# A wider recurrence, a moved product and a later turning in the mixer of a decoder layer

## The chip, the cores and the metric

The kernel runs on one core of a Trainium2 chip. The metric is the device time of one launch in microseconds (us), the median of several runs. Profiles come from one profiled execution. TensorE does the matrix products (PE; its weight loads are shown as PEld), VectorE (DVE) and ScalarE (ACT) the elementwise work, GpSimd (POOL) a few clearings and sums, and SyncE (SP) issues nearly all transfers.

## The reference

One layer of a decoder over 512 tokens of width 2048, all float32. After an RMSNorm one projection feeds three mixers, whose outputs are joined, projected and added; then a SwiGLU block of hidden width 5632 and a last RMSNorm.

```
h = rms_norm(x, attn_norm_g);  proj = h @ w_in
ya = diff_attention(...)            # 4 heads, two softmaxes each, causal
yb = sliding_window_attention(...)  # 8 heads, window 128, sinks
feats = token_shift(rw, mu)         # 16 heads of 64
kk = kk / max(norm(kk), 1e-12);  k = k * (1 + (a - 1) * k_a)
step:  S = S * w_t + (S @ a_t) b_t' + v_t k_t';  y_t = S r_t     # a_t = -kk, b_t = kk * a
x = x + concat(ya, yb, yc) @ w_out
x = x + (silu(gate) * up) @ w_down
return rms_norm(x, final_norm_g)
```

## The kernel before

**Dense work.** Every projection works on tiles of 128 output features by 512 tokens. Its weights come in 512 KB pieces (`raw`), are rounded on ScalarE to a high part (`wh`, L207) and on VectorE to the rest (`wl`, L208), and three matmuls a step (L130) make the product. The weights of a projection are loaded while the one before it runs. Projections go in a fixed order: r, k, v for eight pairs of heads (k first), then q, k, v for four attention heads, with `kb` and `vb` of the window attention ahead of the third head, then `qb`, then the output projection `po` and the feed-forward block (`pg`, `pu`, `pd`).

**Lanes and the planner.** The mixers' own instructions are written as generators in lanes. After each dense matmul `pump` lets each lane whose due time has come go on by one piece. Due times are in the planner's own time `self.now`, which each matmul advances by an estimate; `charge` adds up estimated VectorE and ScalarE time in `self.free` and `self.last`. A bare `yield` means "when the last piece should be done, plus `slack`", `yield 2.5` means 2.5 us of planned time later. TensorE's order is exactly the order so written. VectorE's and ScalarE's order is set by a scheduler by priority, in which `high_priority` moves instructions ahead. Where the next dense projection needs a tile whose older content is still to be used, `need` lets only the lanes run until it is free.

**A pair's way.** For each pair of heads hp:

- `rates`: decay and rate tiles `W`, `V` (`IW`), `a`.
- `prep`: the norm of kk (`kn` matmul), kk (L512), `ar[:, :, 0]` (L518), kk*a (L521), two writes of `bk` (L526), a*k (L527), two more (L531). Then it waits until `loop{hp-2}` is done (the gate, L534), transposes `bk` on TensorE (`bt`, L134) into `bkn`, takes r, writes `ar[:, :, 1]` (L547), and forms the masked products `gr`, `zl` and `L` (`linv`, L574). `ar` has two buffers, so that of pair hp is the one of pair hp-2. The diagonal 32x32 blocks of `L` go to memory (`li`, L585).
- `inverse`: 32 blocks come back, one in each of 32 partitions as a 32x32 matrix `x` (L621). Thirty steps of two VectorE instructions (L629, L630) invert them all. ScalarE makes the transposed copy `xtt` (L633), and both go to memory (`xi`, `xj`).
- `join`: the inverses come back into `L` (L649), two transposed ones into `xn` (L651); two rounds of small matmuls (`pt`, `po`) and ScalarE copies fill the off-diagonal block.
- `chain` (named `loop{hp}`): eight chunks in sequence, each with z, u, S and y matmuls and copies between them. Then `post` (named `chain{hp}`).

The next pair's `prep` begins when the one before is done, and a loop begins when the y tile of the one before is free. Two tiles are released late: the dense v of pair hp may be stored only when v of pair hp-1 has been used up.

**Attention.** `diff_head` begins with `chain7` done. For each of four blocks `scores` makes two score matmuls (`sa`), softmax on VectorE and ScalarE into `pa`; `turned` transposes it on TensorE (`wt`); `values` multiplies (`oa`). Blocks are staggered: `scores(blk + 2)` is issued after `turned(blk)`. A tile of the third head's q may be stored only when head 0 is done.

Of the kernel before, what the change touches and what calls it, by code (L numbers as in the profile page):

```python
# [8 lines left out]
F32 = mybir.dt.float32  # L9
F32R = mybir.dt.float32r  # L10
AF = mybir.ActivationFunctionType
ALU = mybir.AluOpType
AX = mybir.AxisListType

P = 128
T = 512
# [3 lines left out]
C = 64  # L20
NCH = T // C
# [67 lines left out]
class Kernel:  # L89
    def __init__(self, tc, ins, out, dbg=None, stop=None):  # L90
        self.tc = tc
        self.nc = tc.nc
        self.i = ins
        self.out = out
        self.dbg = dbg or {}
        self.stop = stop
        self.lanes = [[], [], [], [], [], [], [], []]
        self.order = [self.lanes[j] for j in (2, 7, 6, 5, 0, 1, 3, 4)]
        self.done = set()
        self.flags = set()  # L100
        self.now = 0.0
        self.due = {}
        self.free = {"DVE": 0.0, "Activation": 0.0}
        self.last = 0.0
        self.slack = 0.3

    def col(self, name, j=0, n=P):
        c = COL[name] + j
# [384 lines left out]
    def prep(self, hp):  # L493
        nc, rp = self.nc, self.rp
# [5 lines left out]
        k = q["k"]  # L500
# [4 lines left out]
        ps = self.pm.tile([P, T], F32, tag="m", name=f"kn{hp}")  # L505
        self.mm(ps, self.cst("onesbd", P), rn, start=True, stop=True)
        kk = rp.tile([P, T], F32, tag="kk", name=f"kk{hp}")

        nc.scalar.activation(kk, ps, AF.Relu, bias=self.cst("knmin", 1))
        nc.scalar.activation(kk, kk, AF.Ln, bias=self.cst("kneps", 1))  # L510
        nc.scalar.activation(kk, kk, AF.Exp, scale=-0.5)
        nc.vector.scalar_tensor_tensor(out=kk, in0=k, scalar=kk_g, in1=kk, op0=ALU.mult, op1=ALU.mult)  # L512

        def c3(x):
            return x.rearrange("p (n c) -> p n c", c=C)

        ar = rp.tile([P, NCH, 2, C], F32, tag="ar", name=f"ar{hp}", bufs=2)
        nc.vector.scalar_tensor_tensor(out=ar[:, :, 0, :], in0=c3(kk), scalar=-1.0, in1=W[:, :, 0:64],  # L518
                                       op0=ALU.mult, op1=ALU.mult)
        bk = rp.tile([P, NCH, 2, C], F32, tag="bk", name=f"bk{hp}")  # L520
        nc.vector.tensor_tensor(out=kk, in0=kk, in1=a, op=ALU.mult)  # L521
        nc.scalar.activation(a, a, AF.Identity, bias=self.one_less("k_a", hp), scale=self.col("k_a", hp))

        for h in range(2):
            s = slice(h * 64, h * 64 + 64)
            nc.vector.tensor_tensor(out=bk[s, :, h, :], in0=c3(kk)[s], in1=V[s, :, 1:65], op=ALU.mult)  # L526
        nc.vector.tensor_tensor(out=a, in0=a, in1=k, op=ALU.mult)  # L527
        self.done.add(f"k{hp}")
        for h in range(2):
            s = slice(h * 64, h * 64 + 64)  # L530
            nc.vector.tensor_tensor(out=bk[s, :, 1 - h, :], in0=c3(a)[s], in1=V[s, :, 1:65], op=ALU.mult)  # L531
        yield

        while hp >= 2 and f"loop{hp - 2}" not in self.done:  # L534
# [9 lines left out]
        while "r" not in q:  # L544
            yield
        r = q["r"]
        nc.vector.tensor_tensor(out=ar[:, :, 1, :], in0=c3(r), in1=W[:, :, 1:65], op=ALU.mult)  # L547

        nc.vector.tensor_tensor(out=a, in0=a, in1=r, op=ALU.mult)
# [63 lines left out]
    def inverse(self, q):  # L613

        nc, rp = self.nc, self.rp
        hp = q["hp"]
        yield 2.5


        x = rp.tile([32, 32, 32], F32, tag="i2", name="x")  # L620
        nc.sync.dma_start(out=x, in_=q["li"].rearrange("h b n s t -> (h b n) s t"))  # L621
        yield 2.5
        nc.vector.memset(x.rearrange("p s t -> p (s t)")[:, 0:1024:33], 1.0)
        tmp = rp.tile([32, 32, 32], F32, tag="i3", name="xt")
        for j in range(1, 31):
            n = 31 - j
            cl = x[:, j:j + 1, j + 1:32].to_broadcast([32, j, n])
            rw = x[:, 0:j, j:j + 1].to_broadcast([32, j, n])
            nc.vector.tensor_tensor(out=tmp[:, :j, :n], in0=cl, in1=rw, op=ALU.mult)  # L629
            nc.vector.tensor_tensor(out=x[:, 0:j, j + 1:32], in0=x[:, 0:j, j + 1:32], in1=tmp[:, :j, :n], op=ALU.add)  # L630
            yield max(self.free["DVE"] - self.now - 1.0, 0.1)
        xt = rp.tile([32, 32, 32], F32, tag="i1", name="xtt")
        nc.scalar.copy(out=xt[0:32].rearrange("p t s -> p s t"), in_=x)  # L633
        d = self.dp.tile([2, 2, NCH, 32, 32], F32, name=f"xi{hp}")
        dt = self.dp.tile([2, 2, NCH, 32, 32], F32, name=f"xj{hp}")
        nc.sync.dma_start(out=d.rearrange("h b n s t -> (h b n) s t"), in_=x)
        nc.sync.dma_start(out=dt.rearrange("h b n t s -> (h b n) t s"), in_=xt)
        q.update(xi=d, xj=dt)
        self.lanes[7].append((f"inv{hp}", self.join(q)))
        yield  # L640

    def join(self, q):

        nc, rp = self.nc, self.rp
        hp, L, blocks, d, dt = (q[n] for n in ("hp", "L", "blocks", "xi", "xj"))
        yield 4.5
        xn = rp.tile([P, NCH, 32], F32, tag="xn", name="xnn")
        for h, b, bl in blocks:
            nc.sync.dma_start(out=L[bl, :, bl], in_=d[h, b].rearrange("n s t -> s n t"))  # L649
            if not b:  # L650
                nc.sync.dma_start(out=xn[bl], in_=dt[h, b].rearrange("n t s -> t n s"))  # L651
        yield 3

        ps = self.pc.tile([P, NCH, 32], F32, tag="c", name="pt")
        for n in range(NCH):
            for h in range(2):
                lo, hi = blocks[2 * h][2], blocks[2 * h + 1][2]
                self.mm(ps[hi, n, :], L[lo, n, hi], xn[lo, n, :], start=True, stop=True)
        pt = rp.tile([P, NCH, 32], F32, tag="pt", name="pts")
        for h in range(2):  # L660
            hi = blocks[2 * h + 1][2]
            nc.scalar.copy(out=pt[hi], in_=ps[hi])
        yield
        ps = self.pc.tile([P, NCH, 32], F32, tag="c", name="po")
        for n in range(NCH):
            for h in range(2):
                lo, hi = blocks[2 * h][2], blocks[2 * h + 1][2]
                self.mm(ps[lo, n, :], pt[hi, n, :], L[hi, n, hi], start=True, stop=True)
        for h in range(2):
            lo, hi = blocks[2 * h][2], blocks[2 * h + 1][2]  # L670
            nc.scalar.copy(out=L[lo, :, hi], in_=ps[lo])
        yield
        self.lanes[2].append((f"loop{hp}", self.chain(q)))
# [165 lines left out]
    def diff_head(self, h, q, vtag):  # L839
# [5 lines left out]
        while "k" not in q:  # L845
            yield
        qT, kT = q["q"], q["k"]
        ws = {}

        def scores(blk):  # L850
            nk = (blk + 1) * P
            ps = [self.pm.tile([P, T], F32, tag="m", name=f"sa{h}_{blk}_{c}") for c in range(2)]
            for c in range(2):
                s = slice(c * 64, c * 64 + 64)
                self.mm(ps[c][:, :nk], qT[s, blk * P:(blk + 1) * P], kT[s, :nk])
            p = rp.tile([P, 2, T], F32, tag=("bk", "i1")[blk % 2], name=f"pa{h}_{blk}")
            st = rp.tile([P, 8], F32, tag="st", name=f"st{h}_{blk}", bufs=3)
            for c in range(2):
                nc.vector.tensor_tensor_reduce(out=p[:, c, :nk], in0=ps[c][:, :nk], in1=bias[:, T - nk:], scale=1.0,
                                               scalar=-3e38, op0=ALU.add, op1=ALU.max, accum_out=st[:, c:c + 1])  # L860
            nc.vector.tensor_scalar(out=st[:, 2:4], in0=st[:, 0:2], scalar1=-1.0, scalar2=None, op0=ALU.mult)
            for c in range(2):
                nc.scalar.activation(p[:, c, :nk], p[:, c, :nk], AF.Exp, bias=st[:, 2 + c:3 + c],
                                     accum_out=st[:, 4 + c:5 + c])
            nc.vector.reciprocal(out=st[:, 6:8], in_=st[:, 4:6])
            nc.vector.tensor_tensor(out=st[:, 7:8], in0=st[:, 7:8], in1=self.nlam, op=ALU.mult)
            nc.vector.tensor_scalar(out=p[:, 1, :nk], in0=p[:, 1, :nk], scalar1=st[:, 7:8], scalar2=None, op0=ALU.mult)
            nc.vector.scalar_tensor_tensor(out=p[:, 0, :nk], in0=p[:, 0, :nk], scalar=st[:, 6:7], in1=p[:, 1, :nk],
                                           op0=ALU.mult, op1=ALU.add)
            ws[blk] = p  # L870

        def turned(blk):
            p = ws[blk]
# [21 lines left out]
        for blk in range(4):  # L895
            turned(blk)
            back = self.last + self.slack - self.now
            if blk:
                values(blk - 1)
            if blk < 2:  # L900
                scores(blk + 2)
            yield back
        values(3)
        o = rp.tile([P, T], F32, tag="sq2", name=f"osq{h}")
        nc.scalar.activation(o, po, AF.Square)
# [371 lines left out]
```

## Time and profile before

| | us |
|---|---|
| median of 3 runs | 2482.63 (2481.53 to 2483.27) |
| profiled execution, its own time | 2481.82 |
| its span | 2480.0 |
| PE busy in the span | 2419.3 |
| DVE busy | 1230.6 |
| ACT busy | 824.2 |

Rows of groups give: line, engine, operation, output <- input by the program's names, shape, count, then busy time, mean ns of one, and idle time before with what ended it. Rows of waits give who waited for whom, us in total, times, longest. Rows in order of time give start, duration, engine, operation, and in brackets the idle time just before with its releaser. A matmul in plain float32 leaves two records. The granted clock is that of TensorE, 1.00 being full speed.

### The profile page before, as it was taken

How to read it: one execution, taken by the hardware profiler on the slowest of the kernel's cores; microseconds unless marked ns; L12 is line 12 of the kernel's file. 1: busy time of each engine (PE TensorE's matmuls, PEld its weight loads, DVE VectorE, ACT ScalarE, POOL GpSimd, SP SyncE). 2: the span in 40 equal slices, each digit the busy share in tenths (PEclk: the TensorE clock that was granted, in tenths of full speed). 3: DMA queues.
4: the chain of work that ended last, by engine and by line, in shares of the span. 5: the costliest groups of instructions: out<-in, count | busy, mean ns of one | idle time of the engine just before them, and what ended most of it. 6: DMA issues, size and time to landing. Idle time of an engine off the chain costs nothing.

```text
span 2480.0 us, 30228 instructions
## 1 busy us (share of the span) xinstructions
PE 2419.3 (98%) x12072; PEld 1921.0 (77%) x12072; DVE 1230.6 (50%) x2113; ACT 824.2 (33%) x1383; POOL 93.0 (4%) x117
## 2 busy tenths in 40 slices
PE   8999999989999999999999999999999999999997
PEld 6776666667677778888888888888888888888887
DVE  7587777776454544434343434343434334343437
ACT  5454555544443433322222222222222222222224
POOL 3000000000000002100000000000000000000006
PEclk9999999999999999999999999999999999999999
DMA  5222221213222423322322223232232322322224
GB/s 175 88 80 72 69 81 49 79 60 96 84 83 79 162 94 128 99 96 95 101 94 101 95 95 101 94 99 97 94 101 94 99 97 94 101 94 99 97 94 136
DMA packets 99054, 238.43 MB, mean 96 GB/s; under 512 B 30426, under 2 KB 39266, under 8 KB 98914
## 3 DMA queue, kind: packets, MB, share of 16 engines
q1 hardware_dynamic: 94018, 229.81, 28.7%
q10 hardware_dynamic: 4896, 6.69, 0.8%
q8 instruction: 95, 1.56, 0.2%
q14 instruction: 45, 0.37, 0.0%
HBM read 224.93 MB, written 11.53 MB: 95 GB/s over the span
## 4 chain that ended last, share of the span: by engine, by line
PE 91%; DVE 6%; ACT 1%; issue 1%; DMA 1%; POOL 0%; SPq 0%; DVEq 0%; ACTq 0%; POOLq 0%
PE pg L130 19%; PE pu L130 19%; PE pd L130 19%; PE po L130 7%; PE pd_k L130 4%; PE pd_r L130 3%; PE pd_v L130 2%; PE pd_va L130 2%; PE pd_qb L130 2%; PE pd_qa L130 2%; PE pd_ka L130 1%; PE z L130 1%; PE pd_l L130 1%; PE y L130 1%; PE gr L130 1%
## 5 line engine op out<-in xcount | busy, mean ns | idle before, releaser
L130 PE MATMUL pd<-al,wh_wd 128*128 128x512 f32 (+1 forms) x768 | 285.3, 371 | 0.5 <-DVE al L1127 0.5
L130 PE MATMUL pd<-ah,wh_wd 128*128 128x512 f32 (+1 forms) x768 | 285.5, 372 | 0.4 <-DVE y L1146 0.4
L130 PE MATMUL pd<-ah,wl_wd 128*128 128x512 f32 (+1 forms) x768 | 285.2, 371 | 0.0
L130 PE MATMUL pu<-x1h,wh_wu 128*128 128x512 f32 x704 | 274.3, 390 | 0.0
L130 PE MATMUL pu<-x1h,wl_wu 128*128 128x512 f32 x704 | 273.9, 389 | 0.0
L130 PE MATMUL pu<-x1l,wh_wu 128*128 128x512 f32 x704 | 273.9, 389 | 0.0
L130 PE MATMUL pg<-x1h,wh_wg 128*128 128x512 f32 x704 | 273.9, 389 | 0.0
L130 PE MATMUL pg<-x1h,wl_wg 128*128 128x512 f32 x704 | 273.9, 389 | 0.0
L130 PE MATMUL pg<-x1l,wh_wg 128*128 128x512 f32 x704 | 273.9, 389 | 0.0
L1146 DVE TENSOR_TENSOR y<-y,pd 128x512 f32<-128x512 f32 (+1 forms) x192 | 122.7, 642 | 207.7 <-PE pd L130 207.6
L207 ACT CAST wh_wd<-raw_wd 128x1024 fp32r<-128x1024 f32 x96 | 100.9, 1052 | 356.9 <-PE pd L130 177.2
L207 ACT CAST wh_wu<-raw_wu 128x1024 fp32r<-128x1024 f32 x88 | 92.7, 1053 | 366.7 <-PE pu L130 144.5
L207 ACT CAST wh_wg<-raw_wg 128x1024 fp32r<-128x1024 f32 x88 | 92.7, 1054 | 362.8 <-PE pg L130 144.9
L208 DVE TENSOR_TENSOR wl_wg<-raw_wg,wh_wg 128x1024 fp32r<-128x1024 f32 x88 | 107.8, 1225 | 171.4 <-ACT wh_wg L207 171.4
L208 DVE TENSOR_TENSOR wl_wu<-raw_wu,wh_wu 128x1024 fp32r<-128x1024 f32 x88 | 107.8, 1225 | 133.4 <-ACT wh_wu L207 133.4
L130 PEld LDWEIGHTS pd<-al,wh_wd 128*128 128x128 f32 x768 | 144.7, 188 | 25.7 <-DVE al L1127 0.8
L130 PEld LDWEIGHTS pd<-ah,wh_wd 128*128 128x128 f32 x768 | 144.7, 188 | 25.5 <-issue 0.5
L130 PEld LDWEIGHTS pd<-ah,wl_wd 128*128 128x128 f32 x768 | 144.7, 188 | 25.0
L130 PEld LDWEIGHTS pu<-x1h,wh_wu 128*128 128x128 f32 x704 | 132.2, 188 | 27.6 <-issue 0.2
L130 PEld LDWEIGHTS pu<-x1l,wh_wu 128*128 128x128 f32 x704 | 132.2, 188 | 27.6 <-issue 0.2
L130 PEld LDWEIGHTS pg<-x1l,wh_wg 128*128 128x128 f32 x704 | 132.2, 188 | 27.4
L130 PEld LDWEIGHTS pg<-x1h,wh_wg 128*128 128x128 f32 x704 | 132.2, 188 | 27.4
(340 smaller groups left out, 4155.1 us busy)
## 6 DMA issues: line engine op xcount, KB each, us to landing
raw_wd<-in_w_down SPq DMA_DIRECT2D x96, 512.0 KB, 3.2
raw_wg<-in_w_gate SPq DMA_DIRECT2D x88, 512.0 KB, 3.7
raw_wu<-in_w_up SPq DMA_DIRECT2D x88, 512.0 KB, 3.7
raw_wo<-in_w_out SPq DMA_DIRECT2D x32, 512.0 KB, 3.3
raw_k<-in_w_in SPq DMA_DIRECT2D x16, 512.0 KB, 3.7
raw_r<-in_w_in SPq DMA_DIRECT2D x16, 512.0 KB, 3.9
raw_v<-in_w_in SPq DMA_DIRECT2D x16, 512.0 KB, 3.8
x<-in_xT SPq DMA_DIRECT2D x16, 256.0 KB, 4.6
```

Of the source, the lines that this page charges most:

```text
L130: self.tc.keep_in_program_order(self.nc.tensor.matmul(out, lhsT, rhs, start=start, stop=stop))
L207: nc.scalar.copy(out=hi[:, :kn * m], in_=s)
L208: nc.vector.tensor_tensor(out=lo[:, :kn * m], in0=s, in1=hi[:, :kn * m].bitcast(F32), op=ALU.subtract)
L1146: nc.vector.tensor_tensor(out=o, in0=o, in1=ps, op=ALU.add)
```

## The change

- `prep`: everything from kk to the last write of `bk` is traced under `high_priority(300)`. `ar[:, :, 0]` is written after the gate, beside `ar[:, :, 1]`. kk*a goes to a tile of its own (`kkn`, in the buffer of `rn`), so that kk lives on until then.
- `inverse`: the blocks are loaded four times, into 128 partitions; group g of 32 partitions works on the rows 4i+g of the inverse, in a tile `y` of 8 rows, started as unit rows by POOL. Step j works on j//4+1 rows. There are 31 steps, and the loads are given 3.5 us of planned time, not 2.5. Four stores bring the rows together in memory; the transposed copy and its store are gone.
- `join`: waits 7 us, not 4.5, before it loads the inverses, and 6 us, not 3, after it. The transposed inverse `xn` is made by sixteen 32x32 matmuls against the identity (`px`) and two ScalarE copies, as a round ahead of `pt`.
- `diff_head`: each block's scores note when they should be done (`due`), and the turning of a block waits for that.

```diff
+        self.lead = 300
...
-        ar = rp.tile([P, NCH, 2, C], F32, tag="ar", name=f"ar{hp}", bufs=2)
-        nc.vector.scalar_tensor_tensor(out=ar[:, :, 0, :], in0=c3(kk), scalar=-1.0, in1=W[:, :, 0:64],
-                                       op0=ALU.mult, op1=ALU.mult)
...
-        nc.vector.tensor_tensor(out=kk, in0=kk, in1=a, op=ALU.mult)
+        with self.tc.high_priority(self.lead):
...
+            kkn = rp.tile([P, T], F32, tag="rn", name=f"kn{hp}n")
+            nc.vector.tensor_tensor(out=kkn, in0=kk, in1=a, op=ALU.mult)
...
         r = q["r"]
+        ar = rp.tile([P, NCH, 2, C], F32, tag="ar", name=f"ar{hp}", bufs=2)
+        nc.vector.scalar_tensor_tensor(out=ar[:, :, 0, :], in0=c3(kk), scalar=-1.0, in1=W[:, :, 0:64],
+                                       op0=ALU.mult, op1=ALU.mult)
...
-        x = rp.tile([32, 32, 32], F32, tag="i2", name="x")
-        nc.sync.dma_start(out=x, in_=q["li"].rearrange("h b n s t -> (h b n) s t"))
-        yield 2.5
+        x = rp.tile([P, 32, 32], F32, tag="i2", name="x")
+        y = rp.tile([P, 8, 32], F32, tag="i1", name="xy")
+        nc.gpsimd.memset(yf, 0.0)
+        for g in range(4):
+            gs = slice(32 * g, 32 * g + 32)
+            nc.sync.dma_start(out=x[gs], in_=q["li"].rearrange("h b n s t -> (h b n) s t"))
+            nc.gpsimd.memset(yf[gs, g:256:36], 1.0)
+        yield 3.5
-        for j in range(1, 31):
-            n = 31 - j
+        for j in range(31):
+            n, m = 31 - j, j // 4 + 1
+            cl = x[:, j:j + 1, j + 1:32].to_broadcast([P, m, n])
+            rw = y[:, 0:m, j:j + 1].to_broadcast([P, m, n])
+            nc.vector.tensor_tensor(out=tmp[:, :m, :n], in0=cl, in1=rw, op=ALU.mult)
+            nc.vector.tensor_tensor(out=y[:, 0:m, j + 1:32], in0=y[:, 0:m, j + 1:32], in1=tmp[:, :m, :n], op=ALU.add)
...
-        nc.scalar.copy(out=xt[0:32].rearrange("p t s -> p s t"), in_=x)
+        for g in range(4):
+            nc.sync.dma_start(out=d[:, :, :, :, g].rearrange("h b n i t -> (h b n) i t"), in_=y[32 * g:32 * g + 32])
...
-        yield 4.5
+        yield 7
...
-        yield 3
+        yield 6
+        ps = self.pc.tile([P, NCH, 32], F32, tag="c", name="px")
+                self.mm(ps[lo, n, :], L[lo, n, lo], self.cst("ident", P)[lo, lo], start=True, stop=True)
+            nc.scalar.copy(out=xn[lo], in_=ps[lo])
+        yield
...
+            due.append(self.last + self.slack)
...
-            yield back
+            yield max(back, due[min(blk + 1, 3)] - self.now)
```

More of the change, by code (lines that the diff above doesn't have):

```diff
@@ L507, in prep @@
         kk = rp.tile([P, T], F32, tag="kk", name=f"kk{hp}")
[L509 to L515, printed above, removed]
-        ar = rp.tile([P, NCH, 2, C], F32, tag="ar", name=f"ar{hp}", bufs=2)
@@ L518, in prep @@
-        nc.vector.scalar_tensor_tensor(out=ar[:, :, 0, :], in0=c3(kk), scalar=-1.0, in1=W[:, :, 0:64],
-                                       op0=ALU.mult, op1=ALU.mult)
-        bk = rp.tile([P, NCH, 2, C], F32, tag="bk", name=f"bk{hp}")
-        nc.vector.tensor_tensor(out=kk, in0=kk, in1=a, op=ALU.mult)
[L522 to L531, printed above, removed]
+        with self.tc.high_priority(self.lead):
+            nc.scalar.activation(kk, ps, AF.Relu, bias=self.cst("knmin", 1))
+            nc.scalar.activation(kk, kk, AF.Ln, bias=self.cst("kneps", 1))
+            nc.scalar.activation(kk, kk, AF.Exp, scale=-0.5)
+            nc.vector.scalar_tensor_tensor(out=kk, in0=k, scalar=kk_g, in1=kk, op0=ALU.mult, op1=ALU.mult)
+            def c3(x):
+                return x.rearrange("p (n c) -> p n c", c=C)
+            kkn = rp.tile([P, T], F32, tag="rn", name=f"kn{hp}n")
+            bk = rp.tile([P, NCH, 2, C], F32, tag="bk", name=f"bk{hp}")
+            nc.vector.tensor_tensor(out=kkn, in0=kk, in1=a, op=ALU.mult)
+            nc.scalar.activation(a, a, AF.Identity, bias=self.one_less("k_a", hp), scale=self.col("k_a", hp))
+            for h in range(2):
+                s = slice(h * 64, h * 64 + 64)
+                nc.vector.tensor_tensor(out=bk[s, :, h, :], in0=c3(kkn)[s], in1=V[s, :, 1:65], op=ALU.mult)
+            nc.vector.tensor_tensor(out=a, in0=a, in1=k, op=ALU.mult)
+            self.done.add(f"k{hp}")
+            for h in range(2):
+                s = slice(h * 64, h * 64 + 64)
+                nc.vector.tensor_tensor(out=bk[s, :, 1 - h, :], in0=c3(a)[s], in1=V[s, :, 1:65], op=ALU.mult)
@@ L617, in inverse @@
         yield 2.5
-        x = rp.tile([32, 32, 32], F32, tag="i2", name="x")
-        nc.sync.dma_start(out=x, in_=q["li"].rearrange("h b n s t -> (h b n) s t"))
-        yield 2.5
-        nc.vector.memset(x.rearrange("p s t -> p (s t)")[:, 0:1024:33], 1.0)
-        tmp = rp.tile([32, 32, 32], F32, tag="i3", name="xt")
-        for j in range(1, 31):
-            n = 31 - j
[L627 to L630, printed above, removed]
-            yield max(self.free["DVE"] - self.now - 1.0, 0.1)
@@ L632, in inverse @@
[L632 to L638, printed above, removed]
+        x = rp.tile([P, 32, 32], F32, tag="i2", name="x")
@@ new lines, in inverse @@
+        y = rp.tile([P, 8, 32], F32, tag="i1", name="xy")
+        yf = y.rearrange("p i t -> p (i t)")
+        nc.gpsimd.memset(yf, 0.0)
[4 more added lines that the diff above has]
+        yield 3.5
+        tmp = rp.tile([P, 8, 32], F32, tag="i3", name="xt")
+        for j in range(31):
[4 more added lines that the diff above has]
+            nc.vector.tensor_tensor(out=y[:, 0:m, j + 1:32], in0=y[:, 0:m, j + 1:32], in1=tmp[:, :m, :n], op=ALU.add)
+            yield max(self.free["DVE"] - self.now - 1.0, 0.1)
@@ L639, in inverse @@
+        d = self.dp.tile([2, 2, NCH, 8, 4, 32], F32, name=f"xi{hp}")
+        for g in range(4):
+            nc.sync.dma_start(out=d[:, :, :, :, g].rearrange("h b n i t -> (h b n) i t"), in_=y[32 * g:32 * g + 32])
+        q.update(xi=d)
         self.lanes[7].append((f"inv{hp}", self.join(q)))
@@ L644, in join @@
         nc, rp = self.nc, self.rp
-        hp, L, blocks, d, dt = (q[n] for n in ("hp", "L", "blocks", "xi", "xj"))
-        yield 4.5
-        xn = rp.tile([P, NCH, 32], F32, tag="xn", name="xnn")
[L648 to L651, printed above, removed]
-        yield 3
+        hp, L, blocks, d = (q[n] for n in ("hp", "L", "blocks", "xi"))
+        yield 7
+        for h, b, bl in blocks:
+            nc.sync.dma_start(out=L[bl, :, bl], in_=d[h, b].rearrange("n i g t -> (i g) n t"))
+        yield 6
+        ps = self.pc.tile([P, NCH, 32], F32, tag="c", name="px")
+        for n in range(NCH):
+            for h in range(2):
+                lo = blocks[2 * h][2]
+                self.mm(ps[lo, n, :], L[lo, n, lo], self.cst("ident", P)[lo, lo], start=True, stop=True)
+        xn = rp.tile([P, NCH, 32], F32, tag="xn", name="xnn")
+        for h in range(2):
+            lo = blocks[2 * h][2]
+            nc.scalar.copy(out=xn[lo], in_=ps[lo])
+        yield
         ps = self.pc.tile([P, NCH, 32], F32, tag="c", name="pt")
@@ L847, in diff_head @@
         qT, kT = q["q"], q["k"]
-        ws = {}
+        ws, due = {}, []
         def scores(blk):
```

## The prediction

> **What bounds the kernel now.** First the page's busy times, then windows cut where the work changes, then the waits of TensorE.
>
> ```profile
> PE 2419.3 (98%) x12072; PEld 1921.0 (77%) x12072; DVE 1230.6 (50%) x2113; ACT 824.2 (33%) x1383; POOL 93.0 (4%) x117
> ```
>
> ```profile
> 1000.00:1500.00 500.00, 500.00 (x2205) 413.78 (x2204) 194.16 (x215) 121.24 (x137) 8.90 (x5) 1.00 0.29 97
> ```
>
> TensorE is the bound, and after 1000 us it has no gap at all and a full clock, so nothing of this change can be won or lost there. What can be won lies in the mixer (columns: width, PE, PEld, DVE, ACT, POOL busy, granted clock, DMA).
>
> ```profile
> 60.00:184.00 124.00, 119.11 (x594) 91.26 (x592) 82.19 (x162) 59.49 (x92) 1.13 (x12) 0.97 0.27 83
> 184.00:361.00 177.00, 167.90 (x1101) 117.54 (x1099) 135.60 (x319) 90.00 (x203) 1.09 (x11) 0.98 0.24 72
> 361.00:383.00 22.00, 20.23 (x170) 14.61 (x170) 11.36 (x25) 10.12 (x25) 0.10 (x1) 0.72 0.26 66
> 383.00:490.00 107.00, 101.65 (x644) 71.07 (x643) 86.63 (x209) 58.60 (x126) 0.71 (x7) 0.99 0.23 70
> 490.00:513.00 23.00, 20.87 (x171) 15.07 (x172) 12.05 (x25) 10.15 (x27) 0.00 (x0) 0.72 0.26 67
> 513.00:662.00 149.00, 143.55 (x964) 101.08 (x963) 95.94 (x242) 69.71 (x169) 0.00 (x0) 0.99 0.26 81
> 662.00:826.00 164.00, 155.49 (x764) 115.23 (x763) 81.60 (x229) 68.42 (x156) 0.00 (x0) 1.00 0.30 98
> ```
>
> Width less PE busy, added over the seven rows, is 37.2 us of idle TensorE; width times (1 - clock) adds 22.4 us of withheld clock. Their sum, 59.6 us, is all that any change of order can bring here. The waits name the idle part:
>
> ```profile
> PE bt L134 <- DVE bk L531: 19.6, 8, 3.6
> ```
>
> ```profile
> PE wt L134 <- DVE pa L868: 6.2, 6, 1.9
> PE gr L130 <- DVE gr L574: 5.7, 6, 2.4
> ```
>
> ```profile
> PE wt L134 <- DVE st L861: 1.2, 1, 1.2
> PE z L130 <- ACT uv L599: 0.9, 1, 0.9
> PE z L130 <- DMA linv<-xi: 0.9, 1, 0.9
> ```
>
> There is a second limit behind the first. In two stretches, 361 to 383 and 490 to 513, no dense projection runs:
>
> ```profile
> 364.36 0.39 PE L130 MATMUL pd_v<-xh,wl_v 128*128 128x512 f32 x1
> ```
>
> ```profile
> 382.93 0.77 PE L130 MATMUL pd_k<-xh,wh_k 128*128 128x512 f32 x1
> ```
>
> For 18.6 us the program holds the next projection back, because storing v5 needs v4 used up, which needs pair 4's preparation, which is gated on the end of loop 2. So the cycle loop, preparation, recurrence, return, loop of pair hp+2 is a latency path that sets the order in which TensorE may proceed; there the small matmuls run at the low clock.
>
> **Part 1: ar behind the gate, preparation ahead of its order.** Today ar's first half stands between kk and bk on VectorE, and its buffer (two of them) is free only when the loop of pair hp-2 has ended:
>
> ```profile
> 142.34 1.22 DVE L208 TENSOR_TENSOR wl_k<-raw_k,wh_k 128x1024 fp32r<-128x1024 f32 x1
> 143.48 1.38 DVE L531 TENSOR_TENSOR bk<-a,IW 64x512 f32<-64x512 f32 x2
> ```
>
> ```profile
> 276.79 0.69 DVE L518 SCALAR_TENSOR_TENSOR ar<-kk,W 128x512 f32<-128x512 f32 x1 [0.42 <-PE y L130]
> ```
>
> ```profile
> 224.32 1.11 PE L134 MATMUL bt<-cc,bk 128*128 128x128 f32 x4 [3.64 <-DVE bk L531]
> ```
>
> ```profile
> 282.40 1.11 PE L134 MATMUL bt<-cc,bk 128*128 128x128 f32 x4 [2.22 <-DVE bk L531]
> ```
>
> At 276.79 ar waits for a y matmul of the older loop; everything for bk (kk*a, two writes, a*k, two writes) queues behind it, the gate opens at the same moment, and the transposes stand 2.2 to 3.6 us. With ar moved, bk of pairs 2 to 7 is complete well before the gate. Pairs 0 and 1 have no gate; there it is queueing (a 1.22 us weight split sits between two bk steps at 142.34), which the priority takes out, while the planner also charges 0.7 us less and brings TensorE earlier: I leave 0.8 us each. So about 18 of 19.6 us go. The other direction: ar's 0.69 us now lies between gate and gram matmuls, 0.7 us per cycle on the latency path. The weight casts and splits that priority pushes back belong to the next projection; no row of the waits shows TensorE waiting for a mixer weight, so I cost that at nothing, bounded by one split (1.22 us) a pair. ScalarE's zl copy moves with ar and stops holding the `a` activation. The new tile kkn takes a buffer that rn has just left; POOL's clearing of that buffer for the next pair waits for kkn instead, and POOL is 4% busy.
>
> **Part 2: the recurrence.** The two instructions of a step over all 240 steps, two of them singly, and where pair 4's pass starts and is stored:
>
> ```profile
> L630 DVE TENSOR_TENSOR x<-x,xt 32x30 f32<-32x30 f32 (+14 forms) x240 | 76.3, 318 | 6.5
> L629 DVE TENSOR_TENSOR xt<-x 32x30 f32<-32x30 f32 (+14 forms) x240 | 76.3, 318 | 6.5
> ```
>
> ```profile
> 256.81 0.18 DVE L629 TENSOR_TENSOR xt<-x 32x30 f32<-32x30 f32 x1
> ```
>
> ```profile
> 334.23 0.40 DVE L630 TENSOR_TENSOR x<-x,xt 32x240 f32<-32x240 f32 x1
> ```
>
> ```profile
> 388.55 0.09 DVE L623 MEMSET x<- 32x32 f32 x1
> ```
>
> ```profile
> 431.30 0.32 SPq L636 DMA_DIRECT2D xi<-x  x1
> ```
>
> ```profile
> 436.27 0.38 SPq L649 DMA_DIRECT2D linv<-xi  x1
> ```
>
> A pass costs (76.3 + 76.3)/8 = 19.1 us of VectorE. From 30 to 240 elements an instruction grows by 0.22 us, 1.05 ns an element, on a fixed 0.15. The new pass has 31 steps with j//4+1 rows of 31-j: 1560 elements in place of 4960, so 62 x 0.15 + 2 x 1560 x 0.00105 = 12.6 us. On 128 partitions instead of 32 I take the same price. The pass lasts 42.8 us (388.55 to 431.30), so it gets 0.45 of VectorE. With that share the new one lasts 28 us: 14.5 saved. If the rest of VectorE's work in that time does not shrink with it, only 6.5 is saved. I take 14.5, since the other work in 383 to 490 (86.6 less two passes) is 0.45 us per us, spread over the stretch, not a fixed amount per pass. Four memsets and a clearing on POOL are hidden in the wait for the loads.
>
> **Part 3: the return.** Planned waits grow by 1.0 + 2.5 + 3.0 us, and the transposed inverse is now made on TensorE rather than copied on ScalarE and loaded from memory:
>
> ```profile
> 316.68 0.69 PE L130 MATMUL pt<-xnn,linv 32*32 32x32 f32 x32
> 317.30 0.50 PE L130 MATMUL pd_k<-xh,wl_k 128*128 128x512 f32 x1
> ```
>
> ```profile
> L633 ACT COPY xtt<-x 32x1024 f32<-32x1024 f32 x8 | 16.2, 2030 | 11.0 <-DVE x L630 10.9
> ```
>
> ```profile
> L662 ACT COPY pts<-pt x16: 362/364/366, 180.1 to 614.4; 32x256 f32<-32x256 f32 x16
> ```
>
> ```profile
> li<-linv SPq DMA_DIRECT2D x32, 32.0 KB, 1.6
> x<-li SPq DMA_DIRECT2D x8, 128.0 KB, 2.4
> ```
>
> Sixteen 32x32 matmuls like pt's hold TensorE 0.62 us: +5.0 us over eight pairs, certain, since nothing hides work on the bounding engine. With two copies like pts' of 0.36 us and the planner's slack of 0.3 the round adds 1.6 us of latency. With the 6.5 planned, the way back is 8.1 longer; ScalarE's 2.03 us copy and two loads go. SP issues four loads for one, four stores for two, and two loads of xnn fewer: three more at 0.32 us, 1 us of its queue, ahead of the next weights. The stores are strided like li's, which land in 1.6 us, well inside the 7 us planned; z's wait on linv<-xi should go.
>
> Net per cycle: -14.5 + 8.1 + 0.7, and 2.9 for bk's wait at the gate: -8.6.
>
> **Part 4: attention's turning.** A head's turning now waits until the next scores are due, while dense matmuls run. Of 7.4 us I keep the first head's:
>
> ```profile
> 675.32 0.66 PE L134 MATMUL wt<-cc,pa 128*128 128x128 f32 x4 [1.86 <-DVE pa L868]
> ```
>
> Head 0 must be finished when the projection qa2 ends, so its wait only moves. -5.5 us.
>
> **The sum, by stage, taking the smaller of what the path and TensorE allow.** Up to 383: the path gives -14.5 + 8.1 - 1.6 (bt's mean wait of 2.4 less the 0.8 left) = -8 for the first loop and -8.6 for the cycle, -16.6; TensorE could give 14.0 idle + 7.3 clock - 1.6 - 2.5 = 17.2. Take -16.5. From 383 to 513: path -8.6, TensorE -14; take -9, with the low clock in the empty stretches worth another -2 if the stretch shortens. From 513 to 662 the projections of attention cover the loops: 5.5 idle + 1.5 clock - 1.2, and 1.8 us of gr's waits I leave standing: -4. Attention -5.5. Together -37. The profiled execution's 2480.0 us of span, with 1.8 us around it, is 0.8 us under the median 2482.6; so 2446.
>
> **The clock, row and rule.**
>
> ```profile
> 280.00:285.00 5.00, 2.78 (x9) 2.24 (x9) 4.92 (x11) 2.04 (x4) 0.10 (x1) 0.69 0.00 0
> 410.00:415.00 5.00, 2.77 (x14) 1.67 (x14) 4.92 (x11) 3.05 (x5) 0.10 (x1) 1.00 0.01 3
> ```
>
> Equal waits of 2.2 us cost clock once and once not, so clock returns only in part. The Trainium skill, TensorE: Matmul & The Clock Gate, "Part 1: The HAM clock gate (the 'warmup' mystery)", says that the clock halves after at least one idle window of about 3.4 us, free-running; by it only the 3.64 us wait could, and the sum would be (b) below. The row at 280 differs from it, and the rows count here.
>
> **Rivals.** (a) The pass saves only its own 6.5 us. A cycle then gains 0.6 and the first loop nothing: -0.6 to 383, -0.6 to 513, then -4 and -5.5: 2472. For it: VectorE is 4.92 of 5 us busy at 280, inside a pass. Against: the other work is spread.
> (b) The clock does not come back with the waits: TensorE then allows 6 less in the first stage, 11 instead of 16.5: 2452. For it: the row at 410. Against: the row at 280. It is also what the clock page of the Trainium skill, named above, would give.
> (c) All covers hold, TensorE is full: 59.6 - 5.0 comes back, 2428. Against: the path of -8.6 a cycle is too slow for it.
> (d) The gates hand the time back: kb and vb wait for chains 6 and 7, and if loops end no earlier, TensorE waits there instead; only attention's 5.5 stays, 2477.
> (e) Slower: small instructions cost what large ones do, so the pass saves nothing and the return's 8.1 stands. First loop +6.5, two cycles +5.9 each, less 4 and 5.5: 2491. It decides when a pass saves less than 2.9 us; against it stands the 0.18 at 256.81.
>
> **Numbers.** Forecast 0.42, own range 2438 to 2457; (a) 0.20; (b) 0.10; (c) 0.08; (d) 0.09; (e) 0.11. A measurement tells 0.2%, 5 us, from nothing: (d) falls half inside it. Faster 0.83, same 0.06, slower 0.11. Range 2434 to 2479, which leaves out (c) and (e).
>
> **What the next profile would show.** Right: no bt wait over 1 us; a pass near 28 us from load to store; both stretches without projections shorter and their clock above 0.8; wt waits under 2 us; 256 more small matmul records at 0.62 us a pair. Wrong: passes over 36 us; z waiting for linv or px for its loads; TensorE waiting at qa2 or vb for a chain.

## The result and the profile after

| | before | changed |
|---|---|---|
| median of the runs on one chip, us | 2482.08 (2479.28 to 2483.27) | 2465.59 (2460.77 to 2467.38) |
| ratio, 95% interval | | 0.9934 [0.9922, 0.9947] |
| profiled execution, us | 2481.82 | 2460.77 |

The change gains 16.5 us where 37 were forecast. The profiled execution is the lowest of the four runs, so its trace shows 21.0 us. First its busy times, then the seven windows of the prediction (width, PE, PEld, DVE, ACT, POOL busy, granted clock, DMA), then TensorE's waits. The order of work is earlier now, so a window does not hold quite the same work as before.

```profile
PE 2415.4 (98%) x12328; PEld 1915.2 (78%) x12328; DVE 1181.9 (48%) x2121; ACT 813.8 (33%) x1391; POOL 99.4 (4%) x157
```

```profile
60.00:184.00 124.00, 115.80 (x647) 87.22 (x645) 75.46 (x170) 58.99 (x103) 1.75 (x15) 0.97 0.28 84
184.00:361.00 177.00, 176.34 (x1299) 122.84 (x1296) 125.54 (x332) 93.72 (x218) 3.43 (x27) 1.00 0.27 78
361.00:383.00 22.00, 21.83 (x142) 14.97 (x141) 19.38 (x60) 14.78 (x37) 0.22 (x2) 1.00 0.19 61
383.00:490.00 107.00, 103.13 (x752) 72.63 (x751) 67.41 (x180) 50.42 (x115) 2.07 (x16) 0.95 0.28 78
490.00:513.00 23.00, 23.00 (x155) 15.69 (x153) 18.12 (x54) 16.43 (x40) 0.00 (x0) 1.00 0.15 47
513.00:662.00 149.00, 145.25 (x993) 102.90 (x994) 81.71 (x225) 63.25 (x157) 0.74 (x5) 0.99 0.30 90
662.00:826.00 164.00, 159.43 (x790) 118.78 (x788) 80.09 (x224) 68.22 (x158) 0.00 (x0) 1.00 0.34 112
```

```profile
PE px L131 <- DMA linv<-xi: 9.7, 7, 2.9
...
PE wt L135 <- DVE pa L881: 2.8, 6, 0.8
PE bt L135 <- DVE bk L531: 2.3, 1, 2.3
PE pd_k L131 <- DVE wl_k L209: 2.2, 1, 2.2
PE wt L135 <- DVE st L874: 1.5, 2, 0.8
```

The windows at 361 and 490, which had a clock of 0.72, now have the full clock, and the empty stretches between projections are gone. From 184 to 361 TensorE stands 0.7 us in 177. But two windows have hardly gained or have lost: 60 to 184 is busy 115.8 us where it was 119.1, and 383 to 490 has a clock of 0.95 where it was 0.99. Both hold one of the new waits, of px for the inverses that come back from memory:

```profile
153.33 0.39 PE L131 MATMUL pd_r<-xh,wh_r 128*128 128x512 f32 x1
156.67 0.28 PE L131 MATMUL px<-cc,linv 32*32 32x32 f32 x2 [2.95 <-DMA linv<-xi]
157.52 1.06 PE L131 MATMUL px<-cc,linv 32*32 32x32 f32 x30 [0.57 <-DMA linv<-xi]
...
467.93 0.31 PE L131 MATMUL px<-cc,linv 32*32 32x32 f32 x2 [2.78 <-DMA linv<-xi]
468.78 1.06 PE L131 MATMUL px<-cc,linv 32*32 32x32 f32 x30 [0.55 <-DMA linv<-xi]
...
471.52 0.63 PE L131 MATMUL pd_r<-xl,wh_r 128*128 128x512 f32 x1
```

```profile
470.00:475.00 5.00, 5.00 (x47) 3.67 (x48) 2.44 (x6) 1.33 (x4) 0.00 (x0) 0.50 0.01 3
```

A wait of px is paid twice: first it stands, then the projection's matmuls behind it take 0.63 us where others take 0.39.

The time from the first matmul of the first pair (pd_k) to the first of the output projection splits into idle time, withheld clock (width times one less the granted clock, in windows of 10 us) and the rest, the work:

| | idle | clock | work | sum |
|---|---|---|---|---|
| before | 37.2 | 22.1 | 708.8 | 768.1 |
| changed | 21.2 | 10.3 | 716.0 | 747.6 |

So 27.8 us came back, and more work took 7.2. (The split is uncertain by some 4 us: the combined kernel at the end has the same matmuls and comes to 712.2 of work.)

Why the inverses come late shows in pair 2's pass (the steps of the recurrence for one pair). SyncE's and VectorE's rows in order of time:

```profile
227.31 1.71 SPq L629 DMA_DIRECT2D x<-li  x4
...
274.28 3.37 SPq L642 DMA_DIRECT2D xi<-xy  x4
```

```profile
225.62 0.41 DVE L577 TENSOR_TENSOR gr<-gr,cc 128x256 f32<-128x256 f32 x1
231.25 1.23 DVE L209 TENSOR_TENSOR wl_v<-raw_v,wh_v 128x1024 fp32r<-128x1024 f32 x1 [5.22 <-ACT wh_v L208]
...
235.46 1.24 DVE L481 TENSOR_TENSOR_SCAN cum<-keep,sg 128x520 f32<-128x520 f32 x1 [1.75 <-ACT sg L377]
...
238.48 0.60 DVE L731 SCALAR_TENSOR_TENSOR uv<-S,D,uv 64x64 f32<-64x64 f32 x2 [1.05 <-PE S L131]
239.11 0.19 DVE L637 TENSOR_TENSOR xt<-x,xy 128x31 f32<-128x31 f32 x1
```

Load to store, from the issue of the blocks' first load to that of the first store of the inverses, is 47.0 us. The first step comes 11.8 us after the load, behind three instructions that wait. Before, the same pair took 51.2 us, with its first step 6.1 us after the load (250.71 to 256.81):

```profile
250.71 0.31 SPq L621 DMA_DIRECT2D x<-li  x1
...
301.92 0.33 SPq L636 DMA_DIRECT2D xi<-x  x1
```

### The profile page after: what moved, and what is told of

It is laid out like the page before. It is cut to its first block, busy times and chain, and to the rows that moved or that the text cites. A ratio compares the mean times of both kernels' runs of the same rounds, so it can differ in the third digit from the quotient of the medians.

```text
span 2459.0 us, 30832 instructions
## 1 busy us (share of the span) xinstructions
PE 2415.4 (98%) x12328; PEld 1915.2 (78%) x12328; DVE 1181.9 (48%) x2121; ACT 813.8 (33%) x1391; POOL 99.4 (4%) x157
## 4 chain that ended last, share of the span: by engine, by line
PE 87%; DVE 2%; ACT 1%; DMA 1%; issue 1%; SPq 0%; POOL 0%; DVEq 0%; ACTq 0%; POOLq 0%
PE pg L131 19%; PE pu L131 19%; PE pd L131 19%; PE po L131 7%; PE pd_v L131 3%; PE pd_k L131 2%; PE pd_r L131 2%; PE pd_va L131 2%; PE pd_qa L131 2%; PE pd_qb L131 2%; PE pd_ka L131 1%; PE y L131 1%; PE z L131 1%; PE S L131 1%; PE pd_kb L131 1%
## 5 line engine op out<-in xcount | busy, mean ns | idle before, releaser
L131 PEld LDWEIGHTS pu<-x1h,wh_wu 128*128 128x128 f32 x704 | 132.1, 188 | 27.6 <-issue 0.2
L131 PEld LDWEIGHTS pu<-x1l,wh_wu 128*128 128x128 f32 x704 | 132.1, 188 | 27.6 <-issue 0.2
L131 PEld LDWEIGHTS pu<-x1h,wl_wu 128*128 128x128 f32 x704 | 132.1, 188 | 27.5
L131 PEld LDWEIGHTS pg<-x1h,wl_wg 128*128 128x128 f32 x704 | 132.1, 188 | 27.4
```

What stands on the lines that cost most here:

```text
L131: self.tc.keep_in_program_order(self.nc.tensor.matmul(out, lhsT, rhs, start=start, stop=stop))
```

## The experiments

The theory at first: each part takes its own wait away, and what is missing went into the return. The rival: the pass of the recurrence did not get short, and the return's planned room (the planned waits of `join`) only covers that.

**Each part alone.** Part 4: the last block of the diff on the kernel before.

```diff
+            due.append(self.last + self.slack)
...
-            yield back
+            yield max(back, due[min(blk + 1, 3)] - self.now)
```

> Only attention's turning waits for its scores; the rest is the kernel before. If the changed kernel's 7.4 to 4.3 us of wt waits is all that this part does: 2479, 3 us under the kernel before, wt waits near 4 us, everything ahead of 660 us as before. As the prediction had it: 5.5 us, 2476.5. Rival, that the freed time is given back where head 0 must be finished: within 1 us of before.

Measured 2475.66 us, 0.9981 [0.9972, 0.9990] of before: 5.2 us. Its wt waits:

```profile
PE wt L134 <- DVE pa L868: 1.8, 2, 1.4
PE wt L134 <- DVE st L861: 1.5, 2, 0.8
```

3.3 us are left of 7.4. This part does what was said of it.

Part 1: `prep` of the changed kernel (priority, `kkn`, ar behind the gate), with the old recurrence and return.

> Only ar behind the gate and the preparation ahead of its order; recurrence, return and attention as before. Theory (each part gives what its waits show): bt's 19.6 us go to under 5, but the two stretches without projections stay, with their low clock, since the recurrence still takes some 43 us a pass: 2466 to 2472. Rival (this part alone is the gain of the whole): 2465 or less and the stretches shorter than 10 us. Second rival (the gates hand the time back): within 4 us of before, stretches longer than 18 us.

Measured 2488.22 us, 1.0034 [1.0021, 1.0047]: 7 us slower, which none of the three expectations had. bt waits 2.9 us, as said, but others come in its place; the second fence is one window of it.

```profile
PE pt L131 <- DMA xnn<-xj: 10.9, 6, 8.6
...
PE z L131 <- DVE uv L723: 5.5, 2, 3.4
PE z L131 <- ACT uv L602: 4.2, 2, 2.2
```

```profile
495.00:526.00 31.00, 20.85 (x166) 14.36 (x164) 12.46 (x30) 10.74 (x26) 0.00 (x0) 0.61 0.22 54
```

One wait for the return, of 8.6 us, falls into a stretch of 31 us without projections at a clock of 0.61. That the plan, with bt early, has no slack left ahead of the return is a reading; no run tests it by itself.

Parts 2 and 3: `inverse` and `join` of the changed kernel, the rest as before.

> Only the recurrence over 128 partitions and the return with its longer planned waits; preparation and attention as before. Theory (the shorter pass ends the stretches without projections, but px waits for its loads): bt waits stay near 19 us, stretches gone, px waits of 5 to 10 us appear: 2474 to 2482. Rival (the return's 8.1 us outweigh the pass): slower than 2485, stretches longer than before.

Measured 2498.99 us, 1.0075 [1.0062, 1.0087]: 18 us slower. Waits:

```profile
PE bt L134 <- DVE bk L531: 22.3, 8, 3.4
PE wt L134 <- DVE pa L878: 7.9, 5, 2.4
...
PE px L130 <- DMA linv<-xi: 6.1, 2, 5.6
```

Load to store takes 40.4 us in place of 47.7 (mean of pairs 2 to 7), store to the loop's first z 25.4 in place of 17.3 (mean of all eight). What the pass gives the return takes, and the px work and its waits come on top: up to the output projection idle time grows by 9.8 us, withheld clock by 3.6, work by 4.4. The rival written down for this run had the time and the reason, but not the longer stretches: the longest without a projection is 8.5 us, where it was 18.2.

Alone the parts make -5, +7 and +18; together -16.5. So they lean on each other, and the planned room was the first suspect.

**The room.** On the changed kernel, then on parts 2 and 3 alone, the two waits of `join` (7 and 6) were changed; the third kernel is the changed one with the old values.

```diff
-        yield 7
+        yield 9        # 4.5 in the other two
...
-        yield 6
+        yield 9        # 3 in the other two
```

> The changed kernel with the return's two planned waits at 9 and 9 us in place of 7 and 6. Theory (the shortfall of the changed kernel is px standing 9.7 us for its loads and the clock that this costs, about 6 us; TensorE is otherwise full and the path has slack): px waits under 1 us, clock at 0.99 in 383 to 490, no stretch without projections over 7 us: 10 to 15 us under the changed kernel, 2451 to 2456. Rival (the waits move, since the loops then start later): px waits gone but stretches without projections come back at v4 or v6, within 4 us of the changed kernel's 2465.6. Second rival (the clock does not come back): 7 to 9 us under it.

Measured 2465.10 us, 0.9937 [0.9924, 0.9949]: no difference to the changed kernel. px still waits 6.5 us, up to 4.3, and a stretch of 29 us without projections has come (515.7 to 544.4). The time is the rival's, though px's waits have not gone. More room is no cure.

> The recurrence over 128 partitions alone (as in the run of the recurrence and return alone, 2499.0), but with the return's planned waits as before, 4.5 and 3 us. Theory (counted from the plan's end of a pass; where VectorE keeps to the plan, the added room is pure delay on the path): from store of the pass to the loop's first z falls from 25.6 us to 19 to 21, time 2480 to 2488. Rival (the loads need the room): px waits grow from 6 to over 15 us and the time stays within 4 us of 2499 or rises.

Measured 2502.18 us, 1.0085 [1.0072, 1.0098]. Store to z is 20.5 us, not 25.4, but px waits 15.8 us, up to 9.2: the rival again.

> The changed kernel with only the return's planned waits put back to 4.5 and 3 us. Theory (with the preparation moved ahead of the pass on VectorE, the pass ends late against the plan and the added room only takes up this lateness): px waits grow from 9.7 to 20 us or more, clock loss with them, 2472 to 2482. Rival (the path alone counts, room is delay): px waits grow by less than 5 us and the loops start some 5 us earlier, 2455 to 2462.

Measured 2514.61 us, 1.0139 [1.0125, 1.0153]: 49 us slower than the changed kernel, 33 us beyond the theory's range, though in its direction. Its waits, and its first px in order of time:

```profile
PE px L131 <- DMA linv<-xi: 47.2, 12, 8.3
```

```profile
148.77 0.39 PE L131 MATMUL pd_k<-xh,wl_k 128*128 128x512 f32 x1
157.26 0.28 PE L131 MATMUL px<-cc,linv 32*32 32x32 f32 x2 [8.11 <-DMA linv<-xi]
```

5.5 us less planned room (4.5 and 3 for 7 and 6) makes px stand 5.2 us longer (8.11 for 2.95) while it starts at nearly the same time, 157.26 and 156.67. The room pays for a lateness; without it the whole gain is lost, and 34 us more.

**The order on VectorE.** First without `high_priority` in `prep`, then with the recurrence's steps raised too.

```diff
-        with self.tc.high_priority(self.lead):
+        with contextlib.nullcontext():
```

> The changed kernel without the priority of the preparation (ar stays behind the gate, kkn stays). Theory (the priority is what makes the passes late, and the wait of pair 1's projection for its weights): px waits under 4 us, wl_k's 2.2 us gone, but bk's waits of pairs 0 and 1 stay near 2.3 us each: within 5 us of 2465.6, since the room then becomes delay. Rival (the priority carries the gain): bt waits over 8 us in total, 2475 or more.

Measured 2461.43 us, 0.9928 [0.9914, 0.9941]. The wait for wl_k is gone, bt waits 4.4 us for 2.3, and the interval overlaps that of the changed kernel: no gain from the priority shows. px still waits 8.6 us, so the priority is not what makes the passes late.

```diff
+            with self.tc.high_priority(self.lead):
-            nc.vector.tensor_tensor(out=tmp[:, :m, :n], ...
-            nc.vector.tensor_tensor(out=y[:, 0:m, j + 1:32], ...
+                nc.vector.tensor_tensor(out=tmp[:, :m, :n], ...
+                nc.vector.tensor_tensor(out=y[:, 0:m, j + 1:32], ...
```

> The changed kernel with the steps of the recurrence under the same priority of 300, so that a pass begins when its loads have landed and not behind the next pair's rates. Theory (the pass with its late start is what keeps the path long: load issue to store 44 us, against 47 before): load issue to store under 36 us, px waits under 2 us, 2450 to 2460. Rival (TensorE is full, the path has slack): pass shorter and px waits gone, but bk, gr or weight splits come late instead, within 4 us of 2465.6.

Measured 2463.49 us, 0.9925 [0.9913, 0.9938]. Load to store stays at 43.3 us, the first step still comes 11.3 us after the load, and px waits 7.7 us. The time is the rival's, its reason is not, since no pass got shorter. This priority does not shorten a pass.

**The pass against the plan.** The planner's own clock, written out while the program is built, tells when it thinks a pass ends. These are numbers of the planner, not of the chip; means over pairs 2 to 7, beside the trace:

| | planned load to store | in the trace | late | time the planner holds projections back |
|---|---|---|---|---|
| before | 45.2 | 47.7 | 2.5 | 29.8 |
| changed | 33.9 | 44.0 | 10.1 | 1.3 |

The planner believes that a pass became 11.3 us shorter; it became 3.7. Of the 7.6 us of new lateness the 5.5 us of new room behind the store cover the most; three waits of px of 2.4 to 3.0 us remain. The next two kernels leave the steps 16 to 30 out, and the planner is charged for them as before, so that TensorE's order is unchanged; the second has the old room as well.

```diff
+            if j < 16:
                 nc.vector.tensor_tensor(out=tmp[:, :m, :n], ...
                 nc.vector.tensor_tensor(out=y[:, 0:m, j + 1:32], ...
+            else:
+                for _ in range(2):
+                    us = 0.14 + m * n * 0.00104
+                    self.free["DVE"] = max(self.free["DVE"], self.now + 0.2) + us
+                    self.last = max(self.free["DVE"], self.last + us + 0.05)
```

> The changed kernel with the steps 16 to 30 of the recurrence left out (so the inverse stays incomplete), while the planner is charged for them as before: the order on TensorE is that of the changed kernel, instruction for instruction, and only VectorE has some 6 us less to do in a pass, which then spreads over some 15 us less. Theory (VectorE's passes end later than the plan thinks, and px waits because of that): px's waits of 9.7 us go to under 2, with the clock behind them; time 2449 to 2457. Rival (px waits for its own transfers, the four stores and four loads, whatever the pass takes): px still waits 7 us or more, 2460 to 2467.

Measured 2439.26 us (2439.00 to 2441.55), 0.9832 [0.9819, 0.9846]: 26 us under the changed kernel, 10 us below even the theory's range. No px wait is among its waits; these are the longest of the mixer:

```profile
PE bt L135 <- DVE bk L531: 2.9, 2, 2.3
PE wt L135 <- DVE pa L887: 2.7, 6, 0.8
PE wt L135 <- DVE st L880: 1.5, 2, 0.8
```

```profile
60.00:184.00 124.00, 120.63 (x696) 90.39 (x695) 76.51 (x157) 63.88 (x117) 1.97 (x17) 1.00 0.30 88
...
383.00:490.00 107.00, 106.45 (x805) 74.50 (x804) 65.34 (x153) 58.51 (x135) 1.24 (x10) 1.00 0.27 78
```

Load to store is 29.3 us, so a pass now ends 4.6 us ahead of the planner's 33.9, not 10.1 behind. Pair 2's pass:

```profile
218.70 1.71 SPq L629 DMA_DIRECT2D x<-li  x4
...
250.77 2.53 SPq L648 DMA_DIRECT2D xi<-xy  x4
```

The two windows that had failed are nearly full (120.6 of 124 us and 106.5 of 107) and at full clock; up to the output projection idle time falls by 11.2 us, withheld clock by 10.3, work stays (716.9). So the late passes, with px's 9.7 us of waits, cost some 20 us, as much as the gain fell short of the forecast. This kernel also spares VectorE 6 us a pass; what that alone is worth no run tells apart.

> The same steps left out of the changed kernel with the old planned room of the return (4.5 and 3 us), the planner still charged for them; with all steps that kernel took 2514.6 us. Theory (the room only has to cover the lateness of the passes): with passes some 15 us shorter px waits under 10 us in place of 47, the stretches without projections close, 2455 to 2475. Rival (the room is needed for the return's own stores and loads, or the plan's uneven order with this room is itself the cost): px still waits 25 us or more and it stays above 2495.

Measured 2442.62 us, 0.9844 [0.9831, 0.9858]: 72 us under the same kernel with all its steps (2514.61), and 12 us below the theory's range. px stands under none of the first nine waits. So the new room is needed for the late passes. That the return by itself would do with the old room this run does not show, since its passes of 27.6 us end early and leave the return more time. The changed kernel tells it nearly: in the three pairs whose px waits longest, the inverses are all back 6.8 to 7.6 us after the store began (150.73 to 157.52, 461.81 to 468.78, 574.70 to 582.27), and the old room is 7.5.

**px's work, doubled,** the planner charged once:

```diff
                 self.mm(ps[lo, n, :], L[lo, n, lo], self.cst("ident", P)[lo, lo], start=True, stop=True)
+                now = self.now
+                self.mm(ps[lo, n, :], L[lo, n, lo], self.cst("ident", P)[lo, lo], start=True, stop=True)
+                self.now = now
```

> The changed kernel with every px matmul done twice into the same place, the planner charged once: 256 more small records on TensorE, all else in the same order. Theory (work on the engine that is the bound is paid in full): TensorE's net work up to the output projection grows by 5.0 (by the prediction's 0.62 us for 32 records) to 7.2 us (what the whole change added), time 2470 to 2474. Rival (the added work falls into waits that stand there anyway, px's own and those behind it): at most 2 us, 2464 to 2468.

Measured 2472.08 us, 0.9964 [0.9951, 0.9977]: 6.5 us over the changed kernel by the medians. The size is the theory's, the place only in part: in its profile work grows by 2.4 us, idle by 1.4 (px waits 11.3), withheld clock by 11.8, in an execution 3 us above its median beside one of the changed kernel 5 us below its own. How the 6.5 us divide is open.

**What the runs point to,** together: the changed kernel without the priority in `prep`, with it on the steps, and with 0.8 us more in `due`.

> A version put together from the runs so far: the changed kernel without the raised priority of the preparation, with the recurrence's steps raised instead, and with 0.8 us more in attention's due times. Theory (each takes its small wait away, wl_k 2.2, some of px's, wt's 4.3, and they add): 2455 to 2460. Rival (a wait taken away here comes back as another, as with each of them alone): 2460 to 2466.

Measured 2458.97 us (2457.66 to 2460.68), 0.9909 [0.9895, 0.9922]: some 6.6 us under the changed kernel, in the theory's range, and the fastest of those that compute everything; the two intervals just touch. The waits did not all add up as the theory had it: px still waits 8.8 us and bt 4.4; the wait for wl_k is gone and wt's are down to 1.1.

## Why the prediction failed, step by step

The direction was right, the size was not: 2465.59 lies in the wide range, outside the forecast's own 2438 to 2457, and nearest to rival (a), 2472. By stage, from the start of pair 6's pd_k (382.93 before), of attention, of its third head and of the output projection, in the profiled executions:

| gain in | forecast | changed | steps 16 to 30 left out |
|---|---|---|---|
| up to 383 | 16.5 | 5.7 | 14.8 |
| 383 to 513 | 11 | 7.1 | 14.6 |
| 513 to 662 | 4 | 1.3 | 6.1 |
| attention | 5.5 | 7.0 | 7.1 |

**The step that failed is Part 2's "I take 14.5".** The instructions were priced rightly:

```profile
L637 DVE TENSOR_TENSOR xt<-x,xy 128x60 f32<-128x60 f32 (+24 forms) x248 | 52.1, 210 | 6.6
L638 DVE TENSOR_TENSOR xy<-xy,xt 128x60 f32<-128x60 f32 (+24 forms) x248 | 52.1, 210 | 7.1
```

(52.1 + 52.1)/8 = 13.0 us a pass, for 12.6; 60 elements on 128 partitions cost 0.22 us, 58 on 32 partitions 0.21. But VectorE's share of a pass did not hold. From the start of the first step to that of the last a pass took 40.3 us (mean of pairs 2 to 7), 19.1 of them its own, a share of 0.47; now 32.2, 13.0 its own, 0.40. What else lies in it is 21.2 and 19.2 us, nearly the same, as the other bound had it. And the first step comes 11.5 us after the load, not 7.1. So of 8.0 us saved between the steps, for 14.5, the later start takes 4.4 back; from load to store 3.7 are left, not even the 6.5 of the lower bound. Rival (a) named the first half of this; the late start nobody had in the sum. And what the sum left out altogether is the plan: it put nothing for passes that end later than the planner thinks.

That the rest of a pass is a fixed amount does not hold in general. With parts 2 and 3 alone a pass takes 29.3 us, 13.1 its own, which is the forecast's share of 0.45; with the steps 16 to 30 left out it takes 17.9, 6.9 its own. The rest is 16.2 and 11.0 us. Why it is 19.2 in the changed kernel is open. The late start comes with the new recurrence: 10.9 us with parts 2 and 3 alone, 6.1 with part 1 alone.

The sum behind the pass held as far as can be seen. From load to the loop's first z (mean of all pairs) it takes 64.6 us before, 61.2 now, and 58.0 with the steps left out: 6.6 less, where -14.5 + 8.1 makes -6.4. There the gains by stage come out at 42.6 us against 37. But load to store is 18.4 us shorter there, more than 14.5, and VectorE has less to do, so this supports the sum and does not test it.

Two slips in the prediction did not decide. The sum reckoned 28 us from the pass's first instruction (388.55), the sign "a pass near 28 us from load to store" from the load, which lies 5.2 us earlier (383.30). And TensorE's 17.2 us for the first stage leave out the row 361 to 383 (1.8 idle, 6.2 clock); the path's 16.6 was the smaller either way.

**Part 3.** "Well inside the 7 us planned" judged the return from the store on, and there it holds:

```profile
x<-li SPq DMA_DIRECT2D x32, 128.0 KB, 2.8
...
xi<-xy SPq DMA_DIRECT2D x32, 32.0 KB, 2.3
linv<-xi SPq DMA_DIRECT2D x32, 32.0 KB, 2.0
```

The store itself was late against the plan. z's wait for linv went, as said, but px, one step earlier, waits 9.7 us, for which the sum had nothing. SyncE's queue paid more than the 0.32 us an issue of the sum: pair 2's four loads took 1.7 us, its four stores 3.4. The 8.1 us of longer return exist with parts 2 and 3 alone (25.4 for 17.3); in the changed kernel the lateness eats them, 17.6 us. px's work was near what was said: 0.69 us a pair at full clock makes 5.5, for 5.0; doubling it cost 6.5 in all.

**Part 1.** bt was nearly right (2.3 us left, all in one pair, for 1.6 in two), and gr's waits, left standing in the sum, went too. The splits, costed "at nothing, bounded by one split (1.22 us) a pair", cost 2.2 us in one pair, more than the bound. The part was summed as a gain of its own; alone it loses 7 us, and its longest wait is one for the return.

**Part 4** was right: 5.2 us alone, for 5.5.

**The other rivals.** (b) is out: 11.8 us of clock came back in the profiled run, and all 22.1 where px does not wait. (c): with the steps left out it came to 2439, still 11 short of it. (d): no gate of attention waits. (e) did not come for its reason, since small instructions are cheap (0.17 to 0.24 us); but two of the three runs of parts alone did end slower. The sign "passes over 36 us" and the sign "px for its loads" both appeared, as the prediction had them for its failure.

## What to carry to other kernels

Where an order is planned ahead, a shorter piece of work counts twice: on the engine, and in the planner's belief. Compare the two before pricing it; a pass that the planner takes for 11 us shorter and that is 4 us shorter starts everything behind it early into waits. To know what one suspected length is worth, leave half its work out while the plan still pays for it, and ask what else that sets free.

## What was not expected of the hardware

A wait of 2.2 us between projection matmuls (140.13, for wl_k) cost no clock (1.00 from 135 to 145), while px's of 2.4 us, with small matmuls behind it, did:

```profile
579.42 0.48 PE L131 MATMUL pd_ka<-xh,wl_ka 128*128 128x512 f32 x1
582.27 1.04 PE L131 MATMUL px<-cc,linv 32*32 32x32 f32 x32 [2.37 <-DMA linv<-xi]
583.24 0.80 PE L131 MATMUL pd_ka<-xh,wh_ka 128*128 128x512 f32 x1
```

```profile
585.00:590.00 5.00, 5.00 (x75) 3.24 (x74) 0.00 (x0) 3.56 (x8) 0.00 (x0) 0.83 0.22 85
```

Here 3.3 us pass between two projection matmuls (579.90 to 583.24); around the wait at 467.93 it is 5.8 us (465.15 to 470.93). The Trainium skill, TensorE: Matmul & The Clock Gate, "Part 1: The HAM clock gate (the 'warmup' mystery)", has the clock fall after at least one idle window of about 3.4 us. That agrees with the 5.8 us, and nearly with the 3.3, if the small matmuls hardly count as busy; no run here separates them from the wait, so it stays a reading.
